# Three reorderings in a diffusion-layer kernel: operands of the seven-product scheme, adding transfers of weight sums, and the fetch of context tokens

## The chip, the core and the metric

The kernel runs on one core of a Trainium2 chip. The core has a matrix engine (PE, with its weight loads shown as PEld), a vector engine (DVE), a scalar engine (ACT), a general engine (POOL), and SP, which here only issues transfers. All work in on-chip memory of 128 partitions; matrix products land in eight accumulation banks of 128 x 512 floats. Each engine works through its own queue in order; engines wait for one another by semaphores. The metric is the device time of one execution in microseconds; lower is better. Everything is float32 in and out.

## The reference

One layer works on 1024 latent tokens and 256 context tokens of width 1024 (`D_FF` is 2816):

```python
x  = x  + 0.5 * ml[2] * swiglu(modulate(rms_norm(x,  norm1_g), ml[0], ml[1]), ffn1_w_in, ffn1_w_out)
cx = cx + 0.5 * mc[2] * swiglu(modulate(rms_norm(cx, norm1_g), mc[0], mc[1]), ffn1_w_in, ffn1_w_out)
hx = modulate(rms_norm(x,  norm2_g), ml[3], ml[4])
hc = modulate(rms_norm(cx, norm2_g), mc[3], mc[4])
# hx @ w_in -> convolution gates and values, q, k, v, merge gates; hc @ w_in -> k, v of the context
y_conv = bg * short_conv(cg * vc)
o = attention(q, [k_ctx, k_lat], [v_ctx, v_lat])         # 8 query heads, 2 key heads, one softmax
x = x + ml[5] * ((sig(g1) * (y_conv @ w_bc) + sig(g2) * (o @ w_ba)) @ w_out)
x = x + 0.5 * ml[8] * swiglu(modulate(rms_norm(x, norm3_g), ml[6], ml[7]), ffn2_w_in, ffn2_w_out)
return rms_norm(x, final_g)
# swiglu(h) = (silu(a) * b) @ w_out with a, b = split(h @ w_in);  modulate(h, s, g) = h * (1 + g) + s
# ml, mc: nine vectors each, from silu(c) @ w_mod + b_mod and silu(c_ctx) @ w_mod + b_mod
```

## The kernel before

**Precision.** Each float32 operand is split in two (`split`, line 187): ACT casts the high part, DVE (or POOL) subtracts it to get the low part. A product is then three matmuls (high by high, high by low, low by high; `terms`, line 639, and `step`, line 891).

**Seven products.** The large products run as a 2 x 2 scheme with seven block products instead of eight. There are two forms of it.

`Winograd` (line 466) is for weights that produce columns: the two halves of the first feed-forward layers (`half1`, `fast`) and the mixing projections (`mix`). Its right operands are eight sums of token blocks, `r[0]` to `r[7]`, with four tiles each, made once: `norm0` makes `r1` and `r2` from the first 512 tokens, `norm1` (line 530) makes the others from the last 512. `norm1` is a generator that yields nine times: after the root, after its broadcast, after each of four quarters (which make `r6` and `r5` and the tiles `h12` and `t34`), and after each of three rounds of four casts for `r7`, `r4` and `r3` (line 554). A pair of column blocks needs products 1 and 2 (`first`), 6, 7 and 4 (`second`, line 741), then 5 and 3 (`third`). Products 1 and 2 need only `r1` and `r2`, so for some pairs ahead they are done while `norm1` still makes the rest: in `start` (line 661) for `mix` and `fast`, nine pairs each (`AH2`, `AH3`), and in `start_together` (line 680) for `half1`, twelve pairs (`AH1`). `start` advances the norm by two steps at the first pair, one step each up to the fifth, and three at the sixth, then runs what is left. In the first half, a loop of seven (line 1104) takes one step of `norm1` and two of the started products each. Left operands are made from weights by `lefts` (line 571): SP loads, POOL makes sums, ACT and DVE split. `prefetch(n)` keeps up to n of them ready; `left()` calls `prefetch(4)` and takes one.

`row_products` (line 791) is for the second feed-forward matrices, `ffn1_w_out` and `ffn2_w_out`. Their left operands are weight blocks, the right ones the hidden rows, fetched from memory (`Rows.fetch`) and added and subtracted in place. The order is products 2, 1, 4, 6, 5, 7 and 3, each over six groups (five of two row blocks and one of one). Products 5, 6 and 3 need sums of weight blocks. `sums` (line 844) makes them by groups: SP loads one block into a tile `ws` (`s1`), POOL adds a second block by an adding transfer (`plus`, line 815), ACT negates the result into `s2`, POOL adds a third block, and a fourth after product 6. Before, the loads and first additions are issued at groups 4 to 6 of product 1 and 1 to 3 of product 4; negation and second addition follow at each group of product 4.

**Context tokens.** `fetch_tokens(CC)` (line 1112) loads two tiles `xtok`; ACT squares them, PE transposes them (`turn_tokens`). It stands behind the loop of seven.

**Residual.** Around the first `row_products`, `after1` (line 1289) reads back the latent tokens from memory at the places named in `residual` (line 1287), a dictionary from (product, group) to the tokens read.

**What sets the order.** The program text isn't the order of the queues. A planner places every engine's instructions at build time, by its own estimates: an instruction goes as soon as its inputs and its tile are ready, earlier lines first. Tiles come from pools with a fixed number of slots; `apool` has 38 (`A_BUFS`) and holds tokens, operands `r`, hidden rows and `ws`. Where `strict[0]` is set, or a call is `pinned`, an instruction stays behind the one that the program named last on its engine. The instructions of `sums` are issued so. What the planner has set is fixed when the kernel runs: an engine whose next instruction waits, waits.

Of the kernel before, what the change touches and what calls it, by code (L numbers as in the profile page):

```python
# [35 lines left out]
C0, C1, CC = ("l", 0, 512), ("l", 512, 512), ("c", 0, CT)  # L36
# [13 lines left out]
def tile_dit_layer(  # L50
# [29 lines left out]
    class Engine:  # L80


        def __init__(self, engine):
            self.engine = engine
# [22 lines left out]
    def uniq(s):  # L107
        n_tiles[0] += 1
        return f"{s}_{n_tiles[0]}"

    def atile(name, shape=(P, SLOT), dt=F32):
        return apool.tile(list(shape), dt, tag="A", name=uniq(name))

    def ttile(name, n=512, dt=F32):
        t = tpool.tile([P, 512], dt, tag="t", name=uniq(name))
        return t[:, :n]

    def small(name, n, dt=F32):
        return spool.tile([P, n], dt, tag=f"s{n}_{name}", name=uniq(name))
# [10 lines left out]
    def matmul(out, w, x, start, stop, pinned=False, on=False):  # L130

        inst = pe.matmul(out, w, x, start=start, stop=stop, skip_group_check=on)
        if pinned:
            tc.keep_in_program_order(inst)
# [7 lines left out]
    def load(out, in_, pinned=False):  # L142
        inst = sp.dma_start(out=out, in_=in_)
        if pinned:
            tc.keep_in_program_order(inst)
# [299 lines left out]
    def run(steps, n=None):  # L445

        if n is None:
            for _ in steps:
                pass
        else:  # L450
            for _ in range(n):
                next(steps, None)
# [13 lines left out]
    class Winograd:  # L466
# [6 lines left out]
        def __init__(self, xs, gain, mod, m, pairs, plain=False, ahead=3, side_from=None):  # L473

            self.xs, self.gain, self.mod, self.m, self.plain = xs, gain, mod, m, plain  # L480
            self.r = {i: [None] * 4 for i in range(8)}
            self.side_from = side_from
            self.n_ahead, self.side, self.started, self.n_left = ahead, None, [], 0
            self.n_squares, self.accs, self.rstd1 = {}, {}, None
            self.source, self.ready = self.lefts(pairs, side_from), []

        def keep(self, i, k, src, lo_eng=None):
# [173 lines left out]
        def start(self, norm):  # L661

            for i in range(self.n_ahead):
                t = wpool.tile([P, 2, 512], F32, tag="wh", name=uniq("uc"), bufs=W_BUFS)
                u, c = t[:, 0], t[:, 1]
                act.copy(out=u, in_=self.product(1))
                run(norm, 2 if i == 0 else 1 if i < 5 else 3)
                dve.tensor_add(out=c, in0=u, in1=self.product(2))
                if i < RESIDENT:
                    self.started.append((u, c))  # L670
                else:
                    self.put_aside(t)
            run(norm)

        def put_aside(self, t):
            ucd = dram.tile([P, 2, 512], F32, name=uniq("ucd"))
# [64 lines left out]
        def second(self, u):  # L741

            v, b = ttile("v"), ttile("b")
            dve.tensor_add(out=u, in0=u, in1=self.product(6))
            dve.tensor_add(out=v, in0=u, in1=self.product(7))
            if self.side:
                self.side(0, self.left())
            dve.tensor_sub(out=b, in0=v, in1=self.product(4))
            return v, b

        def third(self, u, v):
# [39 lines left out]
    def row_products(w, rows, add, after=lambda i, k: None, halves=False):  # L791
# [11 lines left out]
        R, groups = P * rows.n, rows.groups  # L803
        s1, s2 = {}, {}

        def block(k, m, lower, right):
            o = k * P + R * lower
            return w[o : o + m * P, 512 * right : 512 * right + 512].rearrange("(a p) n -> p a n", p=P)
# [6 lines left out]
        def plus(t, *kmlr):  # L815
            pool.dma_start(out=t, in_=block(*kmlr), accum_op=ALU.add)
# [14 lines left out]
        def blocks(k):  # L831
            return (rows.t[k, v, c] for v in range(2) for c in range(2))
# [11 lines left out]
        def sums(i, g):  # L844

            n = len(groups)
            if i == 2 and g >= 2 or i == 1 and g < 2:
                k, _ = groups[g - 2 if i == 2 else n - 2 + g]
                _, _, b21, b22 = blocks(k)
                dve.tensor_sub(out=b21, in0=b21, in1=b22)  # L850
            if i == 1 and g or i == 4 and g == 0:
                k, _ = groups[g - 1 if i == 1 else n - 1]
                b11, b12, b21, _ = blocks(k)
                dve.tensor_sub(out=b11, in0=b12, in1=b11)
                dve.tensor_add(out=b21, in0=b21, in1=b11)
            if i == 1 and g >= 3 or i == 4 and g < n - 3:
                k, m = groups[g - 3 if i == 1 else n - 3 + g]
                s1[k] = atile("ws", (P, 2, 512))[:, :m]
                load(s1[k], block(k, m, 0, 1))
                plus(s1[k], k, m, 1, 1)  # L860
            k, m = groups[g]
            b11, b12, _, b22 = blocks(k)
            if i == 4:
                dve.tensor_sub(out=b11, in0=b11, in1=b22)
                s2[k] = atile("ws", (P, 2, 512))[:, :m]
                act.activation(out=s2[k], in_=s1[k], func=AF.Copy, scale=-1.0)
                plus(s2[k], k, m, 0, 0)
            elif i == 6:
                dve.tensor_add(out=b11, in0=b11, in1=b22)
                plus(s2[k], k, m, 1, 0)  # L870
            elif i == 5:
                dve.tensor_sub(out=b12, in0=b22, in1=b12)
# [33 lines left out]
        for i in (2, 1, 4, 6, 5, 7) + (() if halves else (3,)):  # L906
            if i == 1:
                chain = [ps_t(), ps_t(), ps_o(), ps_s()]
            ps = chain if i in (1, 6, 7) else [ps_s() for _ in range(4)]
            for g, (k, m) in enumerate(groups):  # L910
                for e, lr in enumerate(operands(i, k, m)):
                    if e == 0:
                        fetches(i, g)
                    step(i, ps, k + e, *lr)
                strict[0] = True
                sums(i, g)
                strict[0] = False
                after(i, k)
            for o, ch in to[i]:
                for d in range(4):  # L920
                    add(o + d, ch, ps[d])
            after(i, rows.n)
# [23 lines left out]
    def fetch_tokens(ch):  # L946
        s, o, n = ch
        src = x[0] if s == "l" else ctxt[0]
        toks = []
        for j in range(n // P):  # L950
            t = atile("xtok")
            load(t[:], src[o + j * P : o + (j + 1) * P, :])
            toks.append(t)
        return toks

    def turn_tokens(ch, toks, engines=("dve", "act")):

        s, o, n = ch
        for k in range(KD):
            pt = (ps_o if k % 2 else ps_t)(n)  # L960
            for j, t in enumerate(toks):
                transpose(pt[:, j * P : (j + 1) * P], t[:, k * P : (k + 1) * P])
            dst = (xc if s == "c" else xs)(k, ch)
            if engines[k % 2] == "act":
                act.copy(out=dst, in_=pt)
            else:
                dve.tensor_copy(out=dst, in_=pt)
            yield
# [8 lines left out]
    def column_pairs(w, offsets):  # L977
        return [tuple(w[:, o : o + P] for o in ab) for ab in offsets]
# [3 lines left out]
    half1 = Winograd(xs, gain1["l"], modl, 0, column_pairs(ffn1_w_in[0], ffn_offsets), ahead=AH1, side_from=SIDE_FROM)  # L982
# [66 lines left out]
    for k, pt in banks.items():  # L1049
        scaled(k, pt)  # L1050
    run(mod11, 2)
    run(start, 1)
    half1.prefetch(4, lo_engines=(pool, pool))
    banks = {k: ps_t() for k in (6, 7)}
# [46 lines left out]
    norm1 = half1.norm1()  # L1101
    run(norm1, 2)
    run(start, 2)
    for i in range(7):
        run(norm1, 1)
        run(start, 2)
        strict[0] = True
        for ch in (C0, C1):
            for k in range(2 * i, 2 * i + 2) if i < 4 else ():
                sp.dma_start(out=xd[k, :, ch[1] : ch[1] + 512], in_=xs(k, ch))  # L1110
        strict[0] = False
    tx = fetch_tokens(CC)
    ssc = small("rs_a", 2)
    run(token_squares(tx, ssc))
    yc = token_rstd(ssc, 2)
    run(start)
    run(norm1)
    run(turn_tokens(CC, tx))
    load_vectors(1, [
        ("g2", norm2_g[0]), ("g3", norm3_g[0]), ("gf", final_g), ("qg", q_norm_g[0]),  # L1120
# [157 lines left out]
    norms2, norm1, gain2 = mix.norm0(in_place=True), mix.norm1(), {}  # L1278
# [5 lines left out]
            out=xs(d, ch), in0=t, scalar=gate1["l"][:, d : d + 1], in1=xs(d, ch), op0=ALU.mult, op1=ALU.add  # L1284
        )

    residual = {(2, 4): (C0, 0), (1, 6): (C0, 4), (4, 8): (C1, 0), (6, 4): (C1, 4)}

    def after1(i, k):
        def done(ds, ch):  # L1290
# [629 lines left out]
```

## Time and profile before

| what | before |
|---|---|
| median of 3 runs | 2694.13 us (2691.06 to 2698.36) |
| the profiled execution | 2694.38 us, span 2692.6 us |
| mean granted PE clock | 0.994 |
| DVE, ACT, POOL busy | 75%, 43%, 19% of the span |
| read from and written to memory | 296.30 MB and 66.06 MB |

Times within the span start at its beginning. The first half's first layer runs to about 675 us, its row products to about 900, the mixing projections to about 1300, attention and merging to about 2000, and the second half's layer with its row products to the end. "Released by" in a row names what ended an engine's idle time; where it names an engine that had long been done, it was another cause, often a transfer.

### The profile page before, as it was taken

What the parts mean: (1) busy time and instruction counts of PE and PEld (TensorE: products, weight loads), DVE (VectorE), ACT (ScalarE), POOL (GpSimd) and SP (SyncE); (2) the same over time, 40 slices, a digit from 0 to 9 for tenths busy, and PEclk for the clock granted to TensorE, in tenths of its full rate; (3) what the DMA queues carried; (4) which work ended last, traced back from release to release, by engine and by line L of the source; (5) the groups of instructions that cost most, each with busy time, mean ns of one, the idle gap of its engine ahead of it and who ended that gap; (6) DMA issues with size and microseconds to landing.
All of it is one profiled execution on the core that took longest, in us unless ns stands there. A gap on an engine that the chain in (4) does not pass through costs nothing.

```text
span 2692.6 us, 37398 instructions
## 1 busy us (share of the span) xinstructions
PE 2642.8 (98%) x13593; PEld 2234.4 (83%) x13593; DVE 2009.5 (75%) x3356; ACT 1165.8 (43%) x2317; POOL 523.0 (19%) x409
## 2 busy tenths in 40 slices
PE   8999999999999999999999999999999999999998
PEld 5788998888878877888998888877888888888888
DVE  5888888886977899878487666675458876667875
ACT  6633543333444542333244666674236333334443
POOL 1244011221010044232033111000001433230200
PEclk9999999999999999999999999999999999999998
DMA  7655754346974345433212311002524543228731
GB/s 266 212 188 172 231 168 132 113 134 231 289 162 120 125 143 178 128 123 114 98 48 95 102 59 51 17 32 72 172 86 140 188 145 99 82 90 285 184 83 63
DMA packets 369921, 364.85 MB, mean 136 GB/s; under 512 B 27830, under 2 KB 261448, under 8 KB 369736
## 3 DMA queue, kind: packets, MB, share of 16 engines
q1 hardware_dynamic: 360712, 345.17, 39.0%
q0 software_dynamic: 9024, 17.30, 4.0%
q8 instruction: 106, 1.74, 0.3%
q14 instruction: 79, 0.65, 0.1%
HBM read 296.30 MB, written 66.06 MB: 135 GB/s over the span
## 4 chain that ended last, share of the span: by engine, by line
PE 84%; DVE 7%; DMA 4%; issue 3%; ACT 2%; SPq 1%; POOL 0%; DVEq 0%; ACTq 0%; POOLq 0%
PE ps L88 70%; PE po L88 7%; PE pt L88 7%; DMA rawm<-in_w_mod_dram 1%; DVE wl L88 1%; DMA raw<-in_ffn_w_in_dram 1%; DVE macc L88 1%; SPq L88 1%; DMA ws<-in_ffn_w_out_dram 1%; DVE r L88 0%; DVE xb L88 0%; ACT r L88 0%; DVE u L88 0%; DVE ol L88 0%; DVE y L88 0%
## 5 line engine op out<-in xcount | busy, mean ns | idle before, releaser
L88 PE MATMUL ps<-r,wl 128*128 128x512 f32 x5232 | 1210.1, 391 | 12.4 <-ACT wl L88 6.2
L88 PEld LDWEIGHTS ps<-r,wl 128*128 128x128 f32 x5232 | 980.0, 188 | 220.4 <-ACT wl L88 8.1
L88 ACT CAST wl<-s 128x512 fp32r<-128x512 f32 x256 | 158.4, 621 | 331.2 <-PE ps L88 250.7
L88 ACT CAST wl<-raw 128x512 fp32r<-128x512 f32 x286 | 176.8, 621 | 249.9 <-PE ps L88 156.2
L88 POOL TENSOR_TENSOR s<-raw 128x512 f32<-128x512 f32 x64 | 91.8, 1434 | 983.8 <-PE ps L88 346.6
L88 DVE TENSOR_TENSOR wl<-raw,wl 128x512 fp32r<-128x512 f32 x284 | 201.4, 713 | 68.8 <-ACT wl L88 65.6
L88 DVE TENSOR_TENSOR wl<-s,wl 128x512 fp32r<-128x512 f32 x256 | 236.2, 924 | 8.5 <-ACT wl L88 6.8
L88 POOL TENSOR_TENSOR s<-raw,s 128x512 f32<-128x512 f32 x64 | 103.9, 1624 | 366.9 <-DVE wl L88 356.7
L88 DVE SCALAR_TENSOR_TENSOR macc<-rawm,silu_c,macc 128x512 f32<-128x512 f32 x168 | 137.9, 838 | 8.1 <-DMA rawm<-in_w_mod_dram 7.7
L88 PE MATMUL ps<-wh,r 128*128 128x256 f32 x768 | 141.6, 285 | 0.0
L88 DVE TENSOR_TENSOR pts<-pt,pts 128x512 fp32r<-128x512 f32 x160 | 108.9, 687 | 39.4 <-ACT pts L88 38.5
L88 DVE TENSOR_REDUCE m<-ps 128x1 f32<-128x512 f32 (+1 forms) x192 | 111.0, 597 | 30.8 <-PE ps L88 30.0
L88 DVE TENSOR_TENSOR u<-u,ps 128x512 f32<-128x512 f32 x168 | 114.4, 682 | 24.0 <-PE ps L88 23.8
L88 ACT CAST pts<-pt 128x512 fp32r<-128x512 f32 x160 | 93.3, 594 | 88.8 <-PE pt L88 87.0
L88 PE MATMUL ps<-rh,wl 128*128 128x512 f32 x360 | 123.3, 393 | 0.0
L88 ACT CAST rh<-hid 128x512 fp32r<-128x512 f32 x132 | 81.6, 621 | 92.9 <-PE ps L88 76.6
L88 PEld LDWEIGHTS ps<-wh,r 128*128 128x128 f32 x768 | 120.6, 192 | 0.0
L88 ACT CAST wh<-raw 128x512 fp32r<-128x512 f32 (+1 forms) x88 | 69.5, 796 | 103.5 <-PE ps L88 76.7
L88 PE MATMUL po<-pts,vh 128*128 128x512 f32 x256 | 110.5, 437 | 1.5 <-ACT pts L88 1.5
L88 PE MATMUL ps<-wl,r 128*128 128x256 f32 x384 | 108.8, 283 | 0.0
L88 DVE TENSOR_TENSOR rl<-hid,rh 128x512 fp32r<-128x512 f32 x132 | 90.4, 689 | 20.6 <-ACT rh L88 10.6
L88 PE MATMUL ps<-kl,qs 128*128 128x512 f32 x384 | 105.4, 397 | 0.3 <-ACT pc L88 0.3
(298 smaller groups left out, 5076.0 us busy)
## 6 DMA issues: line engine op xcount, KB each, us to landing
raw<-in_ffn_w_in_dram SPq DMA_DIRECT2D x125, 512.0 KB
raw<-in_ffn_w_out_dram SPq DMA_DIRECT2D x72, 512.0 KB
rawm<-in_w_mod_dram SPq DMA_DIRECT2D x128, 256.0 KB
raw<-in_w_in_dram SPq DMA_DIRECT2D x61, 512.0 KB
hid<-hd SPq DMA_DIRECT2D x40, 512.0 KB
ws<-in_ffn_w_out_dram POOLq DMA_DIRECT2D x30, 512.0 KB, 6.7
ucd<-uc SPq DMA_DIRECT2D x22, 512.0 KB
hd<-c SPq DMA_DIRECT2D x38, 256.0 KB
```

The costliest lines, as they stand in the source:

```text
L88: inst = getattr(self.engine, name)(*args, **kw)
```

## The change

Four edits. In `start`, the norm advances by one step per started pair after the first; after the last pair it advances by 9 less the number of pairs, four weight operands are made ready, and the rest of the norm is kept as `late`. `second` takes four steps of `late` between its products 6 and 7, and the rest after product 4. The first half sets `late` in the same way after its loop. In `sums`, the loads and first additions move to groups 2 to 6 of product 1 and group 1 of product 4. `residual` reads the last 512 tokens at products 6 and 5 instead of 4 and 6. The context tokens are fetched at the fourth turn of the loop of seven.

```diff
@@ class Winograd, __init__
-            self.n_squares, self.accs, self.rstd1 = {}, {}, None
+            self.n_squares, self.accs, self.rstd1, self.late = {}, {}, None, iter(())
@@ start
                 act.copy(out=u, in_=self.product(1))
-                run(norm, 2 if i == 0 else 1 if i < 5 else 3)
+                run(norm, 2 if i == 0 else 1)
                 dve.tensor_add(out=c, in0=u, in1=self.product(2))
...
-            run(norm)
+            run(norm, 9 - self.n_ahead)
+            self.prefetch(4)
+            self.late = norm
@@ second
             dve.tensor_add(out=u, in0=u, in1=self.product(6))
+            run(self.late, 4)
             dve.tensor_add(out=v, in0=u, in1=self.product(7))
             if self.side:
                 self.side(0, self.left())
             dve.tensor_sub(out=b, in0=v, in1=self.product(4))
+            run(self.late)
             return v, b
@@ sums
-            if i == 1 and g >= 3 or i == 4 and g < n - 3:
-                k, m = groups[g - 3 if i == 1 else n - 3 + g]
+            if i == 1 and g or i == 4 and g == 0:
+                k, m = groups[g - 1 if i == 1 else n - 1]
                 s1[k] = atile("ws", (P, 2, 512))[:, :m]
                 load(s1[k], block(k, m, 0, 1))
                 plus(s1[k], k, m, 1, 1)
@@ the first half
     for i in range(7):
+        if i == 3:
+            tx = fetch_tokens(CC)
         run(norm1, 1)
         run(start, 2)
...
-    tx = fetch_tokens(CC)
     ssc = small("rs_a", 2)
     run(token_squares(tx, ssc))
     yc = token_rstd(ssc, 2)
     run(start)
-    run(norm1)
+    run(norm1, 1)
+    half1.late = norm1
     run(turn_tokens(CC, tx))
@@ around the first row products
-    residual = {(2, 4): (C0, 0), (1, 6): (C0, 4), (4, 8): (C1, 0), (6, 4): (C1, 4)}
+    residual = {(2, 4): (C0, 0), (1, 6): (C0, 4), (6, 2): (C1, 0), (5, 2): (C1, 4)}
```

## The prediction, before the changed kernel ran

> **What bounds the kernel now.** I read the page first, then the busy time by stretch, then TensorE's timeline where a stretch shows idle time or a low clock, and then the queues in which the awaited instruction stood. On the page PE is busy for 98% of the span:
>
> ```profile
> PE 2642.8 (98%) x13593; PEld 2234.4 (83%) x13593; DVE 2009.5 (75%) x3356; ACT 1165.8 (43%) x2317; POOL 523.0 (19%) x409
> ```
>
> The change adds and removes no matmul. It can gain only where PE idles or has a lower clock, and its three parts point at three such places. In the rows by stretch stand its bounds and length, the busy time with counts of PE, PEld, DVE, ACT and POOL, the granted clock and the DMA share:
>
> ```profile
> 115.00:127.00 12.00, 9.23 (x37) 7.13 (x36) 3.87 (x17) 3.60 (x7) 3.79 (x3) 0.86 0.79 283
> 757.00:775.00 18.00, 13.41 (x48) 10.58 (x47) 7.19 (x12) 6.36 (x11) 4.59 (x4) 0.81 0.76 185
> 940.00:957.00 17.00, 11.93 (x47) 9.44 (x46) 16.81 (x26) 10.99 (x21) 6.75 (x3) 0.90 0.43 152
> 2480.00:2540.00 60.00, 60.00 (x267) 49.67 (x266) 51.39 (x71) 30.43 (x51) 10.63 (x9) 1.00 0.83 208
> ```
>
> PE's timeline at the three places (start, length; in brackets the idle time before and what ended it):
>
> ```profile
> 121.11 0.30 PE L88 MATMUL pt<-ident,xtok 128*128 128x128 f32 x1 [2.77 <-DMA xtok<-in_ctx_dram]
> ...
> 768.77 0.80 PE L88 MATMUL ps<-rl,wl 128*128 128x512 f32 x1 [4.59 <-DVE rl L88]
> ...
> 952.17 4.10 PE L88 MATMUL ps<-r,wl 128*128 128x512 f32 x11 [5.07 <-ACT wl L88]
> ```
>
> 267 matmuls in 60 us are 0.225 us apiece. At that pace the 48 of the stretch from 757 need 10.8 of its 18 us: **7.2 us** are lost. The 47 from 940 need 10.6 of 17: **6.4 us** lost. From 115 it is 2.77 us idle and the clock, 0.14 of 12 us: **4.5 us**. So a wait costs more than its length, since the clock falls with it. Together 18.1 us, the most the change can bring. In the second use of the row products (2480 to 2540) PE is full at clock 1.00; there is nothing to be had there.
>
> **The change part by part.**
>
> *Context tokens.* The issue on SP's queue, the piece of the chain, DVE's and ACT's timelines:
>
> ```profile
> 114.87 1.06 SPq L88 DMA_DIRECT2D xtok<-in_ctx_dram  x2
> 114.87 6.11 DMA xtok<-in_ctx_dram
> 91.13 1.28 DVE L88 TENSOR_TENSOR h<-x,pt 128x512 f32<-128x512 f32 x2
> 121.06 1.06 ACT L88 ACTIVATE sqtok<-xtok 128x1024 f32<-128x1024 f32 x1 [6.53 <-DMA xtok<-in_ctx_dram]
> ```
>
> The reader sees the load land at 121 and PE and ACT start within 0.2 us of it. What it lacked before, as I read it, was two of the 38 slots of `apool`, which the operands `r` take first. Called at step 3 of seven, it stands just ahead of the norm's last quarter, whose first products DVE makes at 91.13. Counted in the code, 28 to 32 slots are taken then (8 of `r1` and `r2`, 4 `uc`, 6 `h12` and `t34`, 6 `r5` and `r6`, 4 of `h0` and x, up to 4 `uc` being written out). So it gets its two at once and lands before 100. Removed: 2.77 us and the clock's 1.7. What is late next: nothing near, as ACT casts the next weights in the 6.5 us in which it now waits. Added: the issue of two loads of 512 KB ahead of weight loads, and two slots less for the operands made next. By my count the pool fills two tiles earlier, and two casts and the first fresh `uc` wait for a release. Bounds: nothing, if slots come free as fast as ACT casts, and 2.7 us, one product of 12 matmuls. I take 0.6, about one cast (3.75 us for seven, below), as PE has the next product meanwhile. Sum **-3.9**, between -4.5 and -1.8.
>
> By the Trainium skill ("TensorE: Matmul & The Clock Gate", Part 1) the clock falls after an idle window of about 3.4 us; a wait of 2.77 us should then cost only itself, and this part would bring 2.2 us. The 0.86 from 115 to 127 speaks against that here.
>
> *Weight sums.* For each of six groups SP loads a block (`ws`), POOL adds one to it by transfer, ACT negates it and POOL adds another. SP's issues, POOL's timeline, ACT's, the piece of the chain, and DVE's:
>
> ```profile
> L88 SPq DMA_DIRECT2D ws<-in_ffn_w_out_dram x6: 383/444/518, 690.6 to 728.5; - x6
> L88 SPq DMA_DIRECT2D x<-xd x8: 319/476/1064, 746.7 to 755.2; - x8
> 704.22 1.36 POOL L88 DMA_DIRECT2D ws<-in_ffn_w_out_dram  x1 [63.94 <-PE ps L88]
> 711.16 1.23 POOL L88 DMA_DIRECT2D ws<-in_ffn_w_out_dram  x1 [5.58 <-issue]
> 722.47 1.21 POOL L88 DMA_DIRECT2D ws<-in_ffn_w_out_dram  x1 [10.07 <-DMA ws<-in_ffn_w_out_dram]
> 731.59 1.23 POOL L88 DMA_DIRECT2D ws<-in_ffn_w_out_dram  x1 [7.91 <-PE ps L88]
> 739.18 1.21 POOL L88 DMA_DIRECT2D ws<-in_ffn_w_out_dram  x1 [6.37 <-issue]
> 746.91 1.22 POOL L88 DMA_DIRECT2D ws<-in_ffn_w_out_dram  x1 [6.51 <-issue]
> 757.20 2.15 POOL L88 DMA_DIRECT2D ws<-in_ffn_w_out_dram  x2 [9.07 <-issue]
> 765.24 1.22 POOL L88 DMA_DIRECT2D ws<-in_ffn_w_out_dram  x1 [5.89 <-issue]
> 757.93 8.24 DMA ws<-in_ffn_w_out_dram
> 766.25 0.63 ACT L88 ACTIVATE ws<-ws 128x512 f32<-128x512 f32 x1 [7.78 <-DMA ws<-in_ffn_w_out_dram]
> 767.42 0.69 DVE L88 TENSOR_TENSOR wh<-ws,wh 128x512 fp32r<-128x512 f32 x1 [10.30 <-ACT wh L88]
> 768.03 0.68 DVE L88 TENSOR_TENSOR rl<-hid,rh 128x512 fp32r<-128x512 f32 x1
> ```
>
> POOL has one full transfer out at a time, a step of 7 to 10 us. Read upwards: PE idles from 764.2 for the last right operand of product 4 (`rl`, 768.03). On DVE it stands behind a weight split of product 6, this behind its cast, this behind the negation of the sixth sum (766.25), whose transfer is eighth in POOL's queue and lands at 766.2. After the change the six first sums have places 1 to 6, and the second additions that product 6 needs first move from places 5 and 7 to 7 and 8. The wait for the sixth sum goes. What is late next is that split's own sum, place 7 now and landing about 765: it must land by 762.2, since a cast (0.62) and two DVE steps (1.37) follow before 764.2. Its gains: the third load, now pinned behind a row fetch and no longer behind a weight load, comes with the first two, so the step from 711.16 is no longer 11.3 but at most 9 (-2.3); the first load stands two row fetches earlier, 1.46 us each at the rate below (-2.9, or 0 if something else held POOL until 704.22); the eight loads of x, beside which the step from 746.91 took 10.3 against 7.7 before, come after the sums (-2.6); the half-size transfer now ahead of it, +0.7, as at 757.93. It lands near 758, four us in time. Added: loads 3 and 4 pass ahead of product 1's first weights:
>
> ```profile
> 650.00:700.00 50.00, 49.65 (x258) 42.30 (x257) 35.82 (x58) 18.89 (x34) 0.00 (x0) 1.00 0.97 359
> 702.11 0.62 ACT L88 CAST wl<-raw 128x512 fp32r<-128x512 f32 x1 [0.51 <-DMA raw<-in_ffn_w_out_dram]
> 705.87 0.69 DVE L88 TENSOR_TENSOR rl<-hid,rh 128x512 fp32r<-128x512 f32 x1
> 706.44 0.39 PE L88 MATMUL pt<-rh,wl 128*128 128x512 f32 x1
> ```
>
> 512 KB at 359 GB/s take 1.46 us, so these weights, cast as they land, come 2.9 us late; DVE's `rl` goes from 705.87 to about 707, and PE, which starts product 1 at 706.44, waits 0 to 1.3 us. I take 0.6. Sum **-6.6**, between -7.2 and 0 (chain no faster). In the second use the full PE hides all of it.
>
> *Operands of products 7, 4 and 3.* The code does less than its label. `norm1` yields nine times; with nine started products, `start` uses up two steps and then one each, `run(norm, 0)` does nothing, and `late` is empty when `second` runs it. In the first half the loop of seven has used it up too. What stays: the twelve casts are named in three portions, with started products 5, 6 and 7, instead of all with 5, and one split of weights is named sooner. ACT's timeline:
>
> ```profile
> 943.73 1.14 ACT L88 CAST r<-nt 128x512 fp32r<-128x512 f32 x2 [2.70 <-DVE nt L88]
> 944.78 3.75 ACT L88 CAST r<-t 128x512 fp32r<-128x512 f32 x7
> 948.42 0.58 ACT L88 COPY uc<-ps 128x512 f32<-128x512 f32 x1
> 948.90 0.62 ACT L88 CAST r<-t 128x512 fp32r<-128x512 f32 x1
> 949.42 2.18 ACT L88 CAST r<-h 128x512 fp32r<-128x512 f32 x4
> 951.50 0.62 ACT L88 CAST wl<-s 128x512 fp32r<-128x512 f32 x1
> ```
>
> Twelve casts stand between the norm's last step and the split `wl<-s` that PE waits for until 952.17. That split is named with the second half of started product 7, still behind all three portions, and the casts still follow the norm's last step. So **0**, between -6.4 (the wait gone) and +2.7 (one product, if a portion slips later).
>
> **Sum.** The profiled execution took 2694.38 us (span 2692.6); the median of the runs shown is 2694.13. 2694.4 - 3.9 - 6.6 - 0 = **2683.9**.
>
> **The rivals.** *POOL's chain gets no faster, and PE waits longer there: the slower side.* Product 6's sums stand later in the queue. If POOL starts at 704.22 as now and its steps take 10.3 us, as at 746.91, place 8 lands at 704.2 + 7 x 10.3 + 0.7 = 777 and PE waits 14.8 us with 2.6 for the clock, 17.4 against 7.2: 2694.4 - 3.9 + 10.2 = 2700.7. It decides from a step of 9.4 us, where the extra wait eats the tokens' 3.9. For it: steps of 9 us at 722.47. Against: 7.3 to 7.7 from 731.59 to 746.91, and x out of the way.
>
> *The transfers only take turns.* Product 1's weights delay PE by the full 2.9 us and its clock falls (1.7): 2683.9 + 4.0 = 2688. For it: DMA share 0.97 before 700. Against: only 1.3 us reach PE by DVE's queue above. By the Trainium skill ("Trainium Kernel Development and Optimization", Key Constraints) the queues of SP, ACT and POOL run on the same DMA engines, so a transfer moved forward displaces another; the 0.97 agrees.
>
> *The tokens bring nothing*, because operands wait for slots as long: 2683.9 + 3.9 = 2688. *The operands work as labelled*: 2683.9 - 6.4 = 2677.5. *Nothing changes on the path*, or half of the chain's wait stays: 2690 to 2694.
>
> **How the numbers follow.** Forecast (2680 to 2687) 0.50; turns 0.12; tokens lost 0.12; operands 0.08; no change or half 0.11; slower 0.07. The range 2678 to 2692 leaves out the slower case and about half each of the operands and of no change. A measurement here tells some 0.3% apart, 8.1 us. Faster needs less than 2686.0: four fifths of the forecast, the operand case, a little of the others: 0.50. Slower needs over 2702.2: the slower case at longer steps, and orders that nobody foresaw: 0.07. Within: 0.43.
>
> **What would show it.** Right: `xtok` loaded before 95 us, no wait of PE on it and full clock from 115 to 127; POOL's additions begin before 704 and six come before the first second addition; no wait of PE near 764; the wait before 952 as long as now, behind twelve casts. Wrong: PE waiting between 98 and 113 on `r` or `uc` (slots), at 706 on `wl` or `rl` (turns), or from 755 to 777 on `rl` behind casts of `ws` (chain). The whole fails if the planner's new order moves weight splits elsewhere.

## The result and the profile after

| what | before | after |
|---|---|---|
| median | 2696.12 us (9 runs, 2691.06 to 2699.90) | 2687.61 us (9 runs, 2683.11 to 2690.34) |
| ratio, 95% interval | | 0.9966 (0.9958 to 0.9975), so 9.2 us less |
| the profiled execution | 2694.38 us, span 2692.6 | 2688.70 us, span 2686.9 |
| mean granted PE clock | 0.994 | 0.993 |

The changed kernel is faster by a little over 0.3%. The forecast was 2683.9 us, with a range from 2678 to 2692. The total lies in the range, but its parts don't add up as forecast. The busy time by stretch of the changed kernel (bounds, length, then busy time with counts of PE, PEld, DVE, ACT and POOL, the granted clock, the DMA share and GB/s) shows the three places of the prediction and two new ones:

```profile
115.00:127.00 12.00, 12.00 (x58) 9.70 (x57) 9.09 (x24) 6.58 (x14) 5.08 (x4) 1.00 0.51 169
696.00:712.00 16.00, 12.94 (x56) 10.05 (x55) 13.23 (x19) 7.55 (x14) 2.44 (x2) 1.00 0.89 252
757.00:775.00 18.00, 18.00 (x81) 14.93 (x80) 17.63 (x26) 7.91 (x14) 3.39 (x3) 1.00 0.85 207
935.00:952.00 17.00, 11.95 (x41) 9.30 (x40) 14.43 (x23) 11.14 (x23) 4.55 (x3) 0.80 0.49 167
1050.00:1068.00 18.00, 15.43 (x55) 11.82 (x54) 17.59 (x26) 3.90 (x7) 7.43 (x6) 0.81 0.38 122
```

The same view of the kernel before, at the two places not shown above (the work at 1050 now stood at 1055 then):

```profile
696.00:712.00 16.00, 16.00 (x72) 13.25 (x71) 13.31 (x20) 7.93 (x14) 2.19 (x2) 1.00 0.84 271
1055.00:1073.00 18.00, 16.15 (x70) 12.74 (x69) 17.44 (x25) 3.53 (x6) 6.53 (x5) 1.00 0.51 165
```

The stalls on the tokens and near 764 are gone: PE is full at clock 1.00 in the first and third rows. Around 700, where PE was full, 56 matmuls instead of 72 fit: the 16 missing ones, at 0.225 us, are 3.6 us lost. Near 1055, 55 matmuls instead of 70 fit: 3.4 us. The wait before the second products (now near 940) is as long as before:

```profile
943.57 11.68 PE L88 MATMUL ps<-r,wl 128*128 128x512 f32 x38 [5.05 <-ACT wl L88]
```

Two of these are read in the queues. The context tokens' two loads on SP's queue, and POOL's adding transfers, as far as the eighth, in the changed kernel:

```profile
87.91 1.61 SPq L88 DMA_DIRECT2D xtok<-in_ctx_dram  x2
```

```profile
690.65 1.36 POOL L88 DMA_DIRECT2D ws<-in_ffn_w_out_dram  x1 [55.27 <-PE ps L88]
700.10 1.23 POOL L88 DMA_DIRECT2D ws<-in_ffn_w_out_dram  x1 [8.09 <-PE ps L88]
...
733.88 1.22 POOL L88 DMA_DIRECT2D ws<-in_ffn_w_out_dram  x1 [6.85 <-ACT wh L88]
739.93 1.21 POOL L88 DMA_DIRECT2D ws<-in_ffn_w_out_dram  x1 [4.82 <-ACT sq L88]
```

The first now starts at 690.65 instead of 704.22, 13.6 us sooner, of which only some 5 come from the work ahead of it having ended sooner. The tokens are now first used near 97, and PE waits there twice, in the first two rows; the third is the kernel before at that place:

```profile
97.07 0.33 PE L88 MATMUL pt<-ident,xtok 128*128 128x128 f32 x1 [0.61 <-DMA xtok<-in_ctx_dram]
98.94 14.59 PE L88 MATMUL ps<-r,wl 128*128 128x512 f32 x56 [1.32 <-ACT uc L88]
```

```profile
98.33 2.07 PE L88 MATMUL ps<-r,wl 128*128 128x512 f32 x4 [2.66 <-ACT uc L88]
```

The two waits are together shorter than the one before. The new waits of PE near 700, and ACT beside them:

```profile
703.11 0.50 PE L88 MATMUL pt<-rh,wl 128*128 128x512 f32 x1 [1.39 <-ACT wl L88]
706.92 0.73 PE L88 MATMUL pt<-rh,wl 128*128 128x512 f32 x2 [1.67 <-DVE wl L88]
```

```profile
702.44 0.62 ACT L88 CAST wl<-raw 128x512 fp32r<-128x512 f32 x1 [0.29 <-DMA raw<-in_ffn_w_out_dram]
...
707.01 0.62 ACT L88 CAST wl<-raw 128x512 fp32r<-128x512 f32 x1 [1.50 <-DMA raw<-in_ffn_w_out_dram]
```

Product 1's first weights are cast as they land, and PE waits for the casts and splits. That is the delay of the "turns" rival of the prediction, though the clock stays at 1.00.

### The profile page after: what moved, and what is told of

Same layout as the page of the kernel before. It is cut to its first block, busy times and chain, and to the rows that moved or that the text cites. A ratio compares the mean times of both kernels' runs of the same rounds, so it can differ in the third digit from the quotient of the medians.

```text
span 2686.9 us, 37399 instructions
## 1 busy us (share of the span) xinstructions
PE 2643.4 (98%) x13593; PEld 2236.0 (83%) x13593; DVE 2007.1 (75%) x3356; ACT 1166.1 (43%) x2317; POOL 521.3 (19%) x409
## 4 chain that ended last, share of the span: by engine, by line
PE 88%; DVE 6%; DMA 2%; ACT 2%; issue 1%; SPq 1%; POOL 0%; DVEq 0%; ACTq 0%; POOLq 0%
PE ps L88 73%; PE po L88 7%; PE pt L88 7%; DMA rawm<-in_w_mod_dram 1%; DVE macc L88 1%; DVE wl L88 1%; SPq L88 1%; DVE xb L88 0%; DVE r L88 0%; ACT r L88 0%; DMA raw<-in_ffn_w_in_dram 0%; DMA xtok<-in_ctx_dram 0%; DVE ol L88 0%; DVE x L88 0%; DVE pts L88 0%
## 5 line engine op out<-in xcount | busy, mean ns | idle before, releaser
L88 PE MATMUL ps<-r,wl 128*128 128x512 f32 x5232 | 1213.4, 392 | 11.6 <-ACT wl L88 6.8
L88 POOL TENSOR_TENSOR s<-raw,s 128x512 f32<-128x512 f32 x64 | 99.8, 1560 | 363.9 <-DVE wl L88 354.4
```

What stands on the lines that cost most here:

```text
L88: inst = getattr(self.engine, name)(*args, **kw)
```

## The experiments

Each kernel below was timed in five rounds beside the kernel before on the same chip, and has one profile. There were three chips, with medians of 2695.29, 2697.99 and 2695.19 us for the kernel before, so kernels are compared by their ratios to it, with 95% intervals; 0.001 is 2.7 us.

### One part at a time

The first is the kernel before with the earlier fetch of the tokens alone:

```diff
     for i in range(7):
+        if i == 3:
+            tx = fetch_tokens(CC)
         run(norm1, 1)
...
-    tx = fetch_tokens(CC)
     ssc = small("rs_a", 2)
```

> The kernel before with one edit, the earlier fetch of the context tokens. Theory (the tokens' own stall is all that it touches, and both its wait and the low clock behind it go): the stretch from 115 to 127 us runs at clock 1.00 with PE full, TensorE's wait on xtok is under 0.8 us, and the time is 4 to 6 us less than before (ratio 0.998). Rival (the operands wait for slots as long as the tokens did): waits on r or uc between 98 and 118, time within 2 us of before.

The second is the kernel before with the edits of `sums` and `residual` alone, as in the diff of the change.

> The kernel before with two edits, the loads and first additions of the weight sums two groups sooner and the residual's reads later. Theory (7.2 us of stall near 764 traded for 3.4 us of waits on the first weights of product 1): PE full from 757 to 775, two waits of 1.5 to 1.9 us between 700 and 706, time 3 to 5 us less than before. Rival 1 (those two waits come from something else in the changed kernel): they are absent here, and the time is 6 to 7.5 us less. Rival 2 (the transfers only take turns): the time is within 1.5 us of before.

The third is the kernel before with the edits of `__init__`, `start` and `second` alone, as in the diff of the change.

> The kernel before with one edit, the steps of the norm in start and second. Theory (the norm is used up before the first pair is finished, so nothing is deferred; only three portions of casts are named apart): the same twelve casts stand ahead of wl<-s, TensorE's wait before the first second products is 5.0 to 5.3 us, the low clock behind it lasts as long or 1 to 2 us longer, and the time is 0 to 3 us more than before, with the longer wait near 1057 seen in the changed kernel. Rival (operands deferred as the edit's name has it): the wait is under 2 us and the time 5 to 7 us less.

| kernel | median, runs | ratio (interval) | in us |
|---|---|---|---|
| tokens alone | 2683.41, 5 | 0.9962 (0.9949 to 0.9974) | -10.2 |
| sums alone | 2691.53, 11 | 0.9990 (0.9981 to 0.9999) | -2.7 |
| operands alone | 2695.21, 11 | 1.0003 (0.9994 to 1.0012) | +0.8 |
| all (the change) | 2687.61, 9 | 0.9966 (0.9958 to 0.9975) | -9.2 |

The token edit alone gives as much as the whole change, more than the 4 to 6 us expected and twice what its own stall can explain. The operands give nothing, as forecast: PE's wait before the second products is 5.06 us there too. The sums alone behave much as their theory said: PE is full from 757 on, and waits of 1.00 and 2.09 us near 712 and 716 make 3.1 us (3.4 expected, between 700 and 706). The gain of 2.7 us (0.3 to 5.1) is at the lower end of the 3 to 5 expected. The surprise stands in the stretch from 740 to 790, which the token edit doesn't touch. Before, with the sums alone, and with the tokens alone:

```profile
740.00:790.00 50.00, 45.41 (x190) 37.04 (x189) 37.43 (x53) 23.36 (x42) 9.59 (x9) 0.93 0.83 196
```

```profile
740.00:790.00 50.00, 50.00 (x221) 41.10 (x220) 39.51 (x56) 24.97 (x43) 9.52 (x9) 1.00 0.85 206
```

```profile
740.00:790.00 50.00, 48.76 (x216) 40.06 (x214) 39.22 (x55) 24.81 (x44) 9.18 (x8) 1.00 0.78 178
```

222 matmuls fill this stretch. The kernel before loses 32 of them, 7.2 us; the token edit alone, with loads and additions of the sums named exactly as before, loses 6, 1.4 us. With the sums alone it loses 1, 0.2 us. So the stall of the weight sums goes with the edit that was meant for it, and nearly goes without it.

### Where POOL's first addition stands in its queue

POOL's timeline with the token edit alone gives the lead:

```profile
694.00 1.36 POOL L88 DMA_DIRECT2D ws<-in_ffn_w_out_dram  x1 [59.16 <-DMA ws<-in_ffn_w_out_dram]
```

It starts when the loaded sum has landed, by the trace's landings 0.65 us after (693.35). Before, the load landed at 698.84 and the addition started at 704.22, 5.4 us after; the row there names PE, but the matmul whose end the program makes it wait for (`po<-h1ch,wl`) had run by 664.3. One difference is left: in the program as built, this transfer is the 188th instruction in POOL's queue before, counting waits, and the 186th with the token edit, since POOL needs two wait instructions fewer. In just this gap the trace has a record of another kind. The DMA queues of the kernel before, from 698.9 to 704.2 (packets, MB, share of 16 engines):

```profile
q1 hardware_dynamic: 1074, 2.04, 99.8%
q14 instruction: 1, 0.01, 0.4%
```

A packet of 8192 bytes of instructions starts at 702.48, with the memory engines full of data. To test the place, two idle instructions were put early into POOL's queue, once into the kernel before (190th) and once into the token kernel (188th again):

```diff
     make_identity(nc, ident[:])
+    spare = const.tile([P, 1], F32, name="spare")
+    for _ in range(2):
+        nc.gpsimd.memset(spare[:], 0.0)
```

> The kernel before with two idle instructions (memsets of one column that nothing reads) early on POOL, so that its first adding transfer is the 190th of its queue instead of the 188th. In the kernel before it starts 5.4 us after the load that it waits for has landed (698.84 to 704.22), in the token kernel, where it is the 186th, 0.65 us after (693.35 to 694.00). Theory (the delay belongs to the place in POOL's instruction stream, not to anything awaited): it starts 0.6 to 0.7 us after the landing, the loss between 750 and 780 falls from 7 to 2 or 3 us, and the time is 3 to 5.5 us less than before. Rival (the tokens' edit freed it, by slots or by traffic): the 5.4 us stay and the time is within 1.5 us of before.

> The kernel with the token edit alone, with the same two idle instructions on POOL, so that the first adding transfer is the 188th again. Theory (place in the stream): it starts 5.3 us after the landing again, 5 to 7 us are lost between 745 and 775, and the time is 4 to 6.5 us less than before instead of 10. Rival (the tokens' edit freed it): start 0.6 us after the landing, time 9 to 11 us less than before.

The starts followed the place: 0.65 us after the landing in the first, 5.6 us in the second. The times did not follow: 2697.73 us, ratio 1.0000 (0.9990 to 1.0011), and 2696.10 us, 0.9994 (0.9986 to 1.0003), gains of 0 and 1.6 us where at least 3 and 4 were expected. These two kernels changed a second thing: the spare tile moves every tile behind it by 32 bytes. So three more kernels take this apart: the same two instructions without a new tile, in both kernels, and a spare tile without the two instructions.

```diff
+    for _ in range(2):
+        nc.gpsimd.memset(ident[:], 0.0)
     make_identity(nc, ident[:])
```

> The kernel before with two more instructions early on POOL that move no tile (it clears the identity's tile three times instead of once), so that its first adding transfer is the 190th of POOL's queue; the earlier try also moved every tile by 32 bytes. Theory (that move cost what the place gained: DMA share 39.9% against 39.0%): the transfer starts 0.6 to 0.7 us after the landing, the loss between 745 and 790 falls from 7 to about 3 us, and the time is 2.5 to 5 us less than before. Rival (the sooner start brings nothing to the whole): start and stall as in the theory, but a time within 1.5 us of before.

> The kernel with the token edit alone and the same two instructions that move no tile: the first adding transfer is the 188th again. Theory (a block of POOL's instructions ends between the 187th and the 188th, and the next block is fetched only when it is reached, behind the data transfers): it starts 5 to 6 us after the landing, a fetch of 8192 bytes lands in that gap, 6 to 8 us are lost between 745 and 790, and the time is 4 to 6 us less than before, where the token edit alone gave 10. Rival (place is without effect, and the 32 bytes alone cost the earlier try its gain): start 0.6 us after the landing and 9 to 11 us less than before.

```diff
     make_identity(nc, ident[:])
+    spare = const.tile([P, 1], F32, name="spare")
+    nc.vector.memset(spare[:], 0.0)
```

> The kernel before with one spare tile of one column among the constants (cleared by DVE), which moves every tile after it by 32 bytes and leaves POOL's queue as it was. Theory (rows of tiles that start 32 bytes off cost the transfers about 2%): DMA share near 39.9% instead of 39.0%, more time lost where TensorE waits for transfers, and 2 to 5 us more than before. Rival (the place of tiles doesn't matter): DMA share within 0.2 points and time within 1.5 us of before.

| kernel | place | start after landing | lost from 740 to 790 | ratio (interval) |
|---|---|---|---|---|
| before | 188 | 5.4 us | 7.2 us | 1 |
| before, two more | 190 | 0.65 us | 3.6 us | 0.9979 (0.9969 to 0.9989) |
| tokens alone | 186 | 0.65 us | 1.4 us | 0.9962 (0.9949 to 0.9974) |
| tokens, two more | 188 | 5.4 us | 5.2 us | 0.9967 (0.9957 to 0.9977) |
| before, tiles moved by 32 bytes | 188 | 5.6 us | 8.6 us | 1.0030 (1.0020 to 1.0041) |

The rows behind the second and fourth lines, first the kernel before with two more instructions:

```profile
740.00:790.00 50.00, 46.76 (x206) 38.36 (x205) 38.01 (x53) 24.93 (x45) 9.29 (x9) 1.00 0.84 199
```

```profile
699.81 1.36 POOL L88 DMA_DIRECT2D ws<-in_ffn_w_out_dram  x1 [59.33 <-DMA ws<-in_ffn_w_out_dram]
```

Then the token kernel with two more:

```profile
740.00:790.00 50.00, 46.65 (x199) 38.12 (x199) 35.56 (x51) 24.03 (x43) 9.43 (x9) 0.97 0.80 190
```

```profile
701.79 1.36 POOL L88 DMA_DIRECT2D ws<-in_ffn_w_out_dram  x1 [63.92 <-PE ps L88]
```

(222 - 206) x 0.225 = 3.6 us, and (222 - 199) x 0.225 = 5.2 us. The place alone, with every other queue in the same order, made the kernel before 5.6 us faster (3.0 to 8.4), a little more than expected. In the token kernel it brought the late start and 3.8 us of the stall back, but the time rose only by 1.3 us, less than the intervals resolve: it is 8.9 us below before (6.2 to 11.6), where the theory had 4 to 6 and the rival, whose start was wrong, 9 to 11. The profiled executions are not typical here: that of this kernel took 2689.99 us, 5.3 more than its median, that of the token kernel 2680.80, 2.6 less. So what the place costs in time is shown for the kernel before alone.

The delay itself is shown to belong to the place: over all fourteen profiles the start is 5.3 to 5.6 us after the landing in the six kernels with place 188, and 0.65 us in the eight with 186 or 190. That it is the wait for the next block of instructions is read from the packet in the gap. In the token kernel with two more it starts at 700.05, between 696.46 and 701.79; in all six it starts 1.7 to 1.9 us ahead of the transfer, and in none of the eight others is there one between landing and start. By the Trainium skill ("Runtime: NRT & Kernel Launch", Instruction fetch mechanics) instructions come in 16 KiB blocks, fetched while the current one runs, at a cost that is mostly hidden; here the record has 8192 bytes, and 5 us were not hidden.

The 32 bytes cost 0.30% (0.20 to 0.41), 8.1 us, more than the 2 to 5 expected. The clearing of the spare tile also moves DVE's queue by one place; but the two pairs above, which leave DVE's queue as it was, differ by 0.0021 and 0.0027 with the tile and without, so the bytes are the likelier cause. Why they cost time, no run shows. The share of the data queue rose as expected; before, and with the tiles moved:

```profile
q1 hardware_dynamic: 360712, 345.17, 39.0%
```

```profile
q1 hardware_dynamic: 360712, 345.17, 39.8%
```

With this, the first pair of kernels agrees with the second within the intervals: 0.9979 and 0.0030 make 1.0009 (measured 1.0000), 0.9967 and 0.0030 make 0.9997 (measured 0.9994).

### The sums one group sooner instead of two

```diff
-            if i == 1 and g or i == 4 and g == 0:
-                k, m = groups[g - 1 if i == 1 else n - 1]
+            if i == 1 and g >= 2 or i == 4 and g < 2:
+                k, m = groups[g - 2 if i == 1 else n - 2 + g]
                 s1[k] = atile("ws", (P, 2, 512))[:, :m]
```

> The changed kernel with the loads and first additions of the sums one group sooner than before instead of two. Theory (the two waits of 1.55 and 1.84 us at 701 and 705 come from weight-sum loads that pass ahead of product 1's first weights, 1.46 us for each 512 KB): one load fewer passes, so the two waits fall from 3.4 to 1.5 to 2 us together, TensorE stays full from 750 to 780, and the time is 1 to 2 us less than that of the changed kernel. Rival (they come from the adding transfers that share the memory engines, whose first one now runs beside these loads): the waits stay at 3 us or more, and the time does not change.

Measured: 2682.07 us, ratio 0.9941 (0.9928 to 0.9955), the lowest ratio of all, 6.7 us below the changed kernel's, though the last two kernels below are not told apart from it. From 690 to 715, where 112 matmuls fit, the changed kernel and then this one:

```profile
690.00:715.00 25.00, 21.94 (x96) 17.50 (x95) 21.71 (x29) 10.60 (x18) 3.80 (x3) 1.00 0.95 282
```

```profile
690.00:715.00 25.00, 24.62 (x109) 20.04 (x108) 21.79 (x31) 10.85 (x20) 3.80 (x3) 1.00 0.94 276
```

The loss falls from 3.6 to 0.7 us, with one wait of 0.38 us left, and from 740 to 790 PE stays full. PE gains more than the theory gave for one load, and its rival falls as the only cause: the first addition runs beside product 1's weights here as well (693.98 to 703.42), and the waits went. It may still have a share. Product 1's first weights land 5.1 us after the weights ahead of them with the tokens alone (696.60), 10.4 us in the changed kernel (702.42) and 9.2 us here (703.18): one load fewer brings 1.3 us, near the 1.46 for 512 KB, and what makes the rest is not shown. Of the other 3.8 us of the 6.7, 2.0 stand near 1055 (183 matmuls from 1035 to 1080 instead of 174), and the rest is not traced.

### Operands that are really deferred

The norm is used up when `second` asks for the rest. The first kernel stops `start` ahead of the casts of `r4` and `r3`, so that they fall inside the first pair:

```diff
-                run(norm, 2 if i == 0 else 1)
+                run(norm, 2 if i == 0 else 1 if i < 6 else 0)
...
-            run(norm, 9 - self.n_ahead)
             self.prefetch(4)
```

> The changed kernel with the norm of start really held back: start takes steps only up to the r7 portion, and the eight casts of r4 and r3 are made inside the first pair. Theory (the weights of product 6 wait on ACT behind operand casts that nobody needs yet): the first wl<-s cast stands behind six or seven operand casts instead of twelve, TensorE's wait near 938 falls from 5.2 to about 2 us, the clock stays near 1.00, and the time is 4 to 6 us less than that of the changed kernel (12 to 15 less than before). Rival (the wait is only passed on: the other six casts now stand ahead of the weights of product 7): two or three waits of together 4 to 5 us within 10 us, the clock falls as before, and the time is that of the changed kernel within 2 us.

2683.94 us, ratio 0.9961 (0.9949 to 0.9974), within the interval of the changed kernel. The wait of 5.05 us became two, 1.94 us on ACT and 1.65 us on DVE, since the planner put `wl<-s` of product 7 behind all eight deferred casts. The rival was nearer. The next kernel, on the token edit alone, also fixes the order: the weights of products 6 and 7 first, then `r7` in program order.

```diff
-                run(norm, 2 if i == 0 else 1 if i < 5 else 3)
+                run(norm, 2 if i == 0 else 1 if i < 5 else 0)
...
-            run(norm)
+            self.prefetch(2)
+            strict[0] = True
+            run(norm, 1)
+            strict[0] = False
+            self.prefetch(4)
+            self.late = norm
...
             dve.tensor_add(out=u, in0=u, in1=self.product(6))
+            run(self.late)
             dve.tensor_add(out=v, in0=u, in1=self.product(7))
```

> The kernel with the token edit alone, and in start the weights of products 6 and 7 readied ahead of the casts of r7 (which keep the program's order), and the casts of r4 and r3 made inside the first pair. Theory (the stall near 938 is nothing but the order on ACT: weights whose sums POOL has ready by 933 stand behind twelve operand casts): TensorE's wait there falls from 5.06 to under 1 us, the clock stays at 1.00 from 925 to 955, and the time is 5 to 7 us less than with the token edit alone, 14 to 17 less than before. Rival (the casts are all needed within the first pair, so the wait only moves to products 7 and 4): waits of together 3 us or more between 933 and 950, and a time within 2 us of the token edit alone.

The last kernel joins this order with the sums one group sooner, on the changed kernel.

> The changed kernel with the sums one group sooner instead of two, and the weights of products 6 and 7 readied ahead of r7's casts, with r4 and r3 inside the first pair. Theory (the two repairs touch different stretches and add up): no wait over 1 us between 700 and 710 nor between 930 and 942, and 18 to 22 us less than before (ratio 0.992 to 0.993). Rival (what is saved near 938 is paid in the pairs after it, as the waits on POOL's sums at 945 and 979 with the token edit hint): 14 to 17 us less, no better than either repair alone.

They gave 2685.45 us, 0.9948 (0.9934 to 0.9962), and 2682.18 us, 0.9952 (0.9938 to 0.9965). Neither differs from its base beyond the intervals (tokens alone 0.9962, one group 0.9941). The first is 3.8 us below its base, which the intervals don't resolve. The last is 12.9 us below before (9.4 to 16.7), not 18 to 22: the two repairs don't add, and its rival was nearer. With the weights first, PE has no wait from 925 to 945, so the wait there was a matter of order on ACT, whose timeline shows the order that was wanted:

```profile
930.19 1.14 ACT L88 CAST r<-nt 128x512 fp32r<-128x512 f32 x2 [2.70 <-DVE nt L88]
931.24 0.58 ACT L88 COPY uc<-ps 128x512 f32<-128x512 f32 x1
931.71 1.14 ACT L88 CAST wl<-s 128x512 fp32r<-128x512 f32 x2
932.75 0.62 ACT L88 CAST wl<-raw 128x512 fp32r<-128x512 f32 x1
```

Where the gain went stands in three stretches. Tokens alone, then the same with the weights first:

```profile
920.00:965.00 45.00, 39.94 (x170) 32.67 (x169) 40.20 (x64) 22.50 (x45) 17.67 (x11) 0.92 0.48 153
965.00:1000.00 35.00, 35.00 (x156) 28.93 (x156) 34.74 (x57) 12.01 (x20) 14.95 (x10) 1.00 0.44 146
1035.00:1080.00 45.00, 42.34 (x186) 34.20 (x185) 40.16 (x60) 13.34 (x24) 12.83 (x10) 1.00 0.49 151
```

```profile
920.00:965.00 45.00, 43.12 (x189) 34.66 (x188) 44.97 (x66) 24.64 (x47) 21.19 (x12) 1.00 0.49 156
965.00:1000.00 35.00, 33.13 (x147) 26.81 (x146) 34.74 (x58) 9.62 (x18) 11.98 (x9) 1.00 0.53 169
1035.00:1080.00 45.00, 42.11 (x179) 33.87 (x178) 40.54 (x63) 13.00 (x23) 11.43 (x10) 0.96 0.56 172
```

From 920 to 965, 19 more matmuls fit (4.3 us). In the next two stretches 9 and 7 fewer do (3.6 us). Its waits over all three are four of 0.8 to 1.0 us, at 946, 948, 979 and 981, and the pair near 1050. At 946 and 948 PE waits for casts that ACT starts when POOL has the sum ready; at 979 and 981 it waits for DVE. PE, arriving sooner, waits for the next work instead. The expected 5 to 7 us were taken from the first stretch alone.

## Why the prediction was right, and where it was not

**The total.** 2687.6 us lies 3.7 above the forecast and inside the range; the gain is 9.2 us where 10.5 were forecast. That it came so near is luck. The tokens alone gave 10.2 instead of 3.9, and the sums and operands on top of them gave nothing (ratio 0.9962 to 0.9966) instead of 6.6. 2687.6 is also the figure of two rivals, "turns" and "tokens lost", each at 2688; the first is half the story, the second is wrong.

**Tokens (-3.9).** Right for their own stall, a little too small in size; what they would do to the weight sums (5.8 us from 740 to 790) was not seen. The loads go out at 87.91 and nothing waits for them near 121. But they landed at 97.02, not before 95, and PE waits 0.61 us for them at 97.07 and then 1.32 us on `uc`. That wait is one of the prediction's signs of being wrong; it was no loss, since the kernel before waits 2.66 us on `uc` there, and from 88 to 115 both hold 100 matmuls, the changed kernel six small ones of the tokens besides. From 112 to 145, 152 matmuls fit when nothing is lost; the six kernels with the late fetch hold 134, 124, 124, 129, 142 and 132, a mean of 131, so about 4.6 us (21 x 33/152) are saved. Of the slot waits that were priced at 0.6, one cast at 116.45 comes after 2.40 us of waiting for a release, and costs PE nothing. How much the clock takes beside the wait itself differs from run to run, as the last section shows.

**Weight sums (-6.6).** The order came as described: six first additions ahead of the second ones, the chain's eighth place at 739.93, landed by 748.00, so the 762 was met with ease and the wait near 764 went. Two steps failed. First, the whole 7.2 us were put down to the sums. The -2.9 for the first load, "or 0 if something else held POOL until 704.22", came out: with the change the load lands at 690.00 and the addition starts at 690.65, 3.4 us sooner than with the tokens alone. But something else did hold POOL before, for 4.7 us of the 13.6: its place in its instruction stream, which the prediction didn't know, and the token edit moved that place. Either edit is nearly enough against the stall. The sums alone leave 0.2 us of it though POOL still starts 5.4 us late, and the tokens alone leave 1.4; so on top of the tokens the edit had only 1.4 us to save. Second, "I take 0.6" for the loads that pass ahead of product 1's weights: it cost 3.6 us, and 0.7 with one load fewer. The weights came not 2.9 but some 5.8 us later than with the tokens alone (the first two at 702.42 and 704.29 against 696.60 and 698.49). The first adding transfer, now sooner too, may share in that, which is not shown.

**Operands (0).** Right, and for the reason given: nothing is deferred, the twelve casts stand ahead of `wl<-s`, and alone the edit measures +0.8 us (-1.6 to +3.2). The bound of -6.4, the gain of a working deferral, was too large a promise: with the wait removed, 4.3 us are gained there and 3.6 given back within 120 us.

**What nobody foresaw.** Near 1055 the changed kernel loses 3.4 us more than before, 174 matmuls instead of 189 from 1035 to 1080. The waits there are for the same weight casts and splits and only 0.7 us longer (1.51 and 1.07 us instead of 0.78 and 1.07); the rest is the clock, 0.81 instead of 1.00 in the stretches shown. The loss varies from 2.5 to 6.8 us over the kernels, also where the change's parts are absent. What makes the clock fall there is open.

## What to carry to other kernels

Time one edit at a time even where the sum comes out as forecast: here one part gave most of what another was meant to give, and a milder version of that other had the lowest ratio. Where an engine starts late after long idle time and everything it waits for has ended, look at the instruction packets among the DMA queues and at its place in its own queue. Before a wait is priced as a gain, find out what the pairs behind it will wait for when PE arrives there sooner.

## What the runs showed of the hardware that was not expected

- POOL's transfer at one place of its queue started 5.3 to 5.6 us after all that it waited for, with the memory engines full (99.8% above) and a packet of instructions in the gap; from this it is inferred that the next block of instructions came late. Two idle instructions put far ahead took the delay away: -0.21% (-0.31 to -0.11) on the kernel before. The reverse on the token kernel brought the delay back, and no change in time that the intervals resolve.
- Moving every tile by 32 bytes made the same order of instructions, but for one more on DVE, 0.30% (0.20 to 0.41) slower.
- The length of a wait doesn't settle what the clock does behind it. Around the tokens the kernel before waits 2.77 us and the clock falls; with two more instructions on POOL it waits 2.66 us and keeps it. The kernel before, then the other:

```profile
112.00:145.00 33.00, 30.23 (x134) 24.27 (x134) 22.14 (x41) 10.02 (x19) 12.76 (x9) 0.95 0.65 223
```

```profile
112.00:145.00 33.00, 30.34 (x142) 24.56 (x141) 22.49 (x43) 10.41 (x21) 14.37 (x9) 1.00 0.65 216
```

  The idle window of about 3.4 us that the Trainium skill gives ("TensorE: Matmul & The Clock Gate", Part 1) fits the second and not the first. Near 1055 the changed kernel waits 1.51 and then 1.07 us, and its clock falls to 0.81 from 1050 to 1068. With the sums one group sooner the waits are longer, and the clock from 1035 to 1080 stays at 1.00:

```profile
1056.81 0.73 PE L88 MATMUL ps<-r,wl 128*128 128x512 f32 x2 [2.27 <-ACT wl L88]
1058.60 3.69 PE L88 MATMUL ps<-r,wl 128*128 128x512 f32 x15 [1.07 <-DVE wl L88]
```

```profile
1035.00:1080.00 45.00, 41.66 (x183) 33.63 (x182) 40.11 (x57) 13.35 (x24) 14.23 (x11) 1.00 0.45 137
```
